# Projection loop of an RWKV block: the bonus products and each tile's last add move from VectorE to GpSimd

## The chip, the cores and the metric

The kernel runs on one core of a Trainium2 chip. The metric is the device time of one execution in microseconds (us); the median of three executions is compared.

## The reference

Two layers of a diffusion transformer for 256 latent and 256 context tokens of width 1024: each layer is half a feed-forward block, a mixer, and a second half of a feed-forward block. The first layer's mixer is RWKV-7, in two directions. What matters here is how its inputs for the scan and for the readout come from the projections:

```
k = xk @ wk;  v = xv @ wv
kk = to_heads(k * k_k);  kk = kk / max(||kk||, 1e-12)
a = sigmoid(a0 + (xa @ a1) @ a2);  g = sigmoid(xg @ g1) @ g2     # for each direction
k_d = k * (1 + (a - 1) * k_a)
...
bonus = sum(r * k_d * r_k, axis=head) * v
out   = (yn * ln_w + ln_b + bonus) * g
```

The second layer's mixer is grouped attention; it lies outside of the change.

## The kernel before

All activations are held as 128 channels by 512 tokens (256 of the context, 256 latent), so a matrix of 1024 channels is eight tiles. Matrices are split into two parts of float32r, and each product is three matmuls (function `mm3`, lines 268 to 270). The split is a copy by ScalarE (`whi`, L260) and a subtraction by VectorE (`wlo`, L261).

The stage that is changed is `rwkv_project` (L656). Its loop has nine turns, `ct` from 0 to 8, and is pipelined by hand: turn `ct` makes the gates, the key and the decay sums of tile `ct` (`gates`, `key`, `sums`), and finishes tile `ct - 1` (`mixed`, `value`). For ScalarE the order is that of the code; the instructions of the other engines are placed by the framework's planner, so on VectorE and TensorE pieces of two turns are interleaved. Each engine then works through its own queue strictly in that order.

What the steps of one turn do, with the lines used below:

- `sums`: two cumulative sums (VectorE, `cum`, L743), two exponentials `p` and `pin` for each direction (ScalarE, L748 and L750), two one-column memsets and two one-column copies of 8 elements, `pc<-p`, by GpSimd (L747, L751), and a DMA of `pc` (L752).
- `mixed`: VectorE forms `kk` (L758), `b` (L763), the scan's operands `ar` (L768, L769), `kd` (L775), the bonus product `pr` = kd x r for each direction (L777), and `bk` (L778, L779). DMAs write `ar` (`far`, L771) and `bk` (`fbk`, L780, L783) to DRAM.
- `value`: the product with wv and the gates' second product (TensorE, `pp`, `gp`), copies of v by ScalarE (L803, L806, L814), DMAs of v (`fv`, L808) and of the gates (`fgl`, L816). Then, for each direction, TensorE sums the bonus product over each head (`bop`, L819, which has `pr` as its moving operand), VectorE multiplies by v (L821) and applies bias and gate (L822). The two directions are added (L824), and the sum goes to DRAM (`bg`, L825).

All DMA writes of this loop, and the load of r (`load_r`, L707), are issued by GpSimd (`put = nc.gpsimd`, L698). The buffer of `ar` is also that of v's copies (pool `f1`, one buffer, tag "ar", L764 and L804), so `ar` of the next tile can't be written before `fv` has left it, and v's copies can't be made before `far` has left it. `r`, `k`, `sq` and `kk` of a tile lie in the same eight pieces as the results of `value`: L821 of direction 0 overwrites `r`. In the last turn (`ct` = 8) the triangular solve of the scan's first tile (`early_solve`, L955; its VectorE steps are L919 to L938) is interleaved with `mixed` and `value`, and the scan stage begins when it is done.

Of the kernel before, what the change touches and what calls it, by code (L numbers as in the profile page):

```python
# [12 lines left out]
ALU = mybir.AluOpType  # L13
# [75 lines left out]
class Net:  # L89
# [566 lines left out]
    def rwkv_project(self):  # L656
        nc, a = self.nc, self.a
# [3 lines left out]
        with ExitStack() as st:  # L661
# [5 lines left out]
            def ft(nm="ft"):  # L667
                return f.tile([128, 520], F32, tag="f", name=nm)[:, 0:T]
# [4 lines left out]
            def fl(p):  # L673
                return p.rearrange("p h t -> p (h t)")

            def o4(t):
                return t.rearrange("p (h c i) -> p h c i", h=2, c=4)

            def o8(t):
                return t.rearrange("p (h c) i -> p h c i", h=2)  # L680
# [4 lines left out]
            def hmm(w, slot, hslot, q0, q1):  # L685

                return (tuple(u[q0:q1, slot] for u in w), tuple(self.hid(HID0 + hslot)[q0:q1, :, i] for i in range(2)))
# [66 lines left out]
            def mixed(ct, bc):  # L754

                z = zs[ct]
                kt, rt, kkt, p65, pin = (z[q] for q in ("k", "r", "kk", "p65", "pin"))
                nc.vector.scalar_tensor_tensor(  # L758
                    out=kkt, in0=kt, scalar=self.vec[:, V_KK, ct:ct + 1], in1=bc, op0=ALU.mult, op1=ALU.mult)
                b = {}  # L760
                for d in range(2):
                    b[d] = ft("b")
                    nc.vector.tensor_tensor(out=o4(b[d]), in0=self.order(kkt, d), in1=o4(z[W_A, d]), op=ALU.mult)  # L763
                ar = f1.tile([128, 2, 2, 4, 2, 64], F32, tag="ar", name="ar")  # L764
                bk = f1.tile([128, 2, 2, 4, 2, 64], F32, tag="bk", name="bk")
                for d in range(2):
                    kk, r = (self.order(q, d) for q in (kkt, rt))
                    nc.vector.tensor_tensor(out=ar[:, :, d, :, 0], in0=kk, in1=o8(p65[d][:, :, 0:64]), op=ALU.mult)  # L768
                    nc.vector.tensor_tensor(out=ar[:, :, d, :, 1], in0=r, in1=o8(p65[d][:, :, 1:65]), op=ALU.mult)  # L769
                    if d:  # L770
                        put.dma_start(  # L771
                            out=self.far[ct].rearrange("p f d x -> p (f d x)"), in_=ar.rearrange("p f d c s i -> p (f d c s i)"))
                    k = self.order(kt, d)
                    kd = ft("kd")
                    nc.vector.tensor_tensor(out=o4(kd), in0=o4(z["asg", d]), in1=k, op=ALU.mult)  # L775
                    pr = z["pr", d] = ft("pr")
                    nc.vector.tensor_tensor(out=self.order(pr, d), in0=o4(kd), in1=r, op=ALU.mult)  # L777
                    nc.vector.tensor_tensor(out=bk[:, :, d, :, 1], in0=o4(b[d]), in1=o4(pin[d]), op=ALU.mult)  # L778
                    nc.vector.tensor_tensor(out=bk[:, :, d, :, 0], in0=o4(kd), in1=o4(pin[d]), op=ALU.mult)  # L779
                put.dma_start(  # L780
                    out=self.fbk[ct, 0:64].rearrange("p f c s i -> p (f c s i)"), in_=bk[0:64].rearrange("p f d c s i -> p (f d c s i)"))
                for e in range(2):
                    put.dma_start(  # L783
                        out=self.fbk[ct, 64:128].rearrange("p f c s i -> p (f c) s i")[:, :, 1 - e],
                        in_=bk[64:128].rearrange("p f d c s i -> p (f d c) s i")[:, :, e])
# [9 lines left out]
            def value(ct):  # L795
                z = zs[ct]
                own, w = z["own"], z["wg"]
                rkb = f2.tile([128, 128], F32, tag="rkb", name="rkb")
                nc.vector.tensor_scalar(
                    out=rkb, in0=cst[:, C_BO:C_BO + 128], scalar1=self.vec[:, V_RK, ct:ct + 1], scalar2=None, op0=ALU.mult)  # L800
                p = self.product(z["wv"], hlv, BOTH, "pp")
                v = own[0]
                nc.scalar.activation(out=v, in_=fl(p), func=AF.Copy)  # L803
                v2 = f1.tile([128, 2, 2, CTX], F32, tag="ar", name="v2")  # L804
                for d in range(2):
                    nc.scalar.activation(  # L806
                        out=v2[:, :, d].rearrange("p f (c i) -> p f c i", c=4), in_=self.order(v, d), func=AF.Copy)
                put.dma_start(out=self.fv[ct], in_=v2)  # L808
                gs = []
                for d in range(2):  # L810
                    p = self.pmm.tile([128, 2, CTX], F32, tag="mm", name="gp")
                    self.mm3(p, [hmm(w, d, W_GA + d, 0, 128), hmm(w, 2, W_GC, 32 * d, 32 * d + 32)])
                    gl = own[6 + d]
                    nc.scalar.activation(out=gl, in_=fl(p), func=AF.Copy, scale=self.vec[:, V_LW + d, ct:ct + 1])  # L814
                    gs.append(p)
                put.dma_start(out=self.fgl[ct], in_=pieces[:, 8 * (ct % 2) + 6:8 * (ct % 2) + 8])  # L816
                for d in range(2):
                    p = self.pmm.tile([128, T], F32, tag="mm", name="bop")
                    nc.tensor.matmul(out=p, lhsT=rkb, rhs=z["pr", d], start=True, stop=True)  # L819
                    t = own[4 + d]  # L820
                    nc.vector.tensor_tensor(out=t, in0=v, in1=p, op=ALU.mult)  # L821
                    nc.vector.scalar_tensor_tensor(  # L822
                        out=t, in0=t, scalar=self.vec[:, V_LB + d, ct:ct + 1], in1=fl(gs[d]), op0=ALU.add, op1=ALU.mult)
                nc.vector.tensor_tensor(out=own[4], in0=own[4], in1=own[5], op=ALU.add)  # L824
                put.dma_start(out=self.bg[ct], in_=own[4])  # L825

            with self.tc.manual_schedule(engines={mybir.EngineType.Activation}):
# [4 lines left out]
                for ct in range(KT + 1):  # L832
# [25 lines left out]
                    if ct:  # L858
                        mixed(ct - 1, bc)
                    if ct + 1 < KT:  # L860
                        load(ct + 1)
                    if ct:
                        value(ct - 1)
# [820 lines left out]
```

## Time and profile before

| | us |
|---|---|
| median of 3 executions | 2347.47 (2346.8 to 2347.53) |
| the profiled execution | 2345.08 |
| its span | 2343.3 |
| mean granted TensorE clock | 0.953 |
| the changed loop, in the span | some 575 to 762 |

The profile is of one execution. TensorE is busy for 93% of the span, VectorE for 65%, ScalarE for 46% and GpSimd for 7%; the last is nearly all in the changed loop and the scan behind it. Times in the rows are microseconds from the start of the span, durations of single instructions are in us or, where marked, ns. An instruction's span on GpSimd is rough, and it contains the time in which the instruction is held.

### The profile page before, as it was taken

The numbers are of one execution on the slowest core, as the hardware profiler recorded it, in microseconds if no ns is written. First come the engines' busy times: TensorE is split into PE (matmuls) and PEld (weight loads), VectorE is DVE, ScalarE is ACT, GpSimd is POOL, SyncE is SP. The second block draws the span as 40 slices with busy tenths as digits, with TensorE's granted clock in tenths as the row PEclk, the third lists the DMA queues.
The fourth block names the chain that finished last, engine by engine and source line by source line (L and its number), as shares of the span: only waits on it lengthen the run. The fifth ranks groups of instructions, "written<-read, shape, count | busy, mean of one in ns | idle before, by whom it ended". The sixth has DMA issues, their size and how long they took to land.

```text
span 2343.3 us, 44872 instructions
## 1 busy us (share of the span) xinstructions
PE 2184.3 (93%) x18548; PEld 1866.8 (80%) x18548; DVE 1515.0 (65%) x2609; ACT 1073.4 (46%) x1912; POOL 156.3 (7%) x224
## 2 busy tenths in 40 slices
PE   6999999897997899998999999989999999998998
PEld 4777889665775788776997788988778898678997
DVE  3798325566888667574699732579983367775554
ACT  3222325445884555555652222564222365555443
POOL 0000000000453222220000000000000000000000
PEclk9999999898998889998999999999999999798999
DMA  7567336542676534332577533567763464103664
GB/s 260 190 219 227 99 99 194 159 142 72 211 260 208 180 99 131 96 103 79 162 232 227 179 99 90 173 193 244 226 197 96 117 179 125 55 20 119 186 178 137
DMA packets 105004, 366.78 MB, mean 157 GB/s; under 512 B 13920, under 2 KB 16224, under 8 KB 102112
## 3 DMA queue, kind: packets, MB, share of 16 engines
q1 hardware_dynamic: 93024, 319.81, 43.6%
q0 software_dynamic: 11776, 44.12, 6.1%
q8 instruction: 145, 2.38, 0.4%
q14 instruction: 59, 0.48, 0.1%
HBM read 331.30 MB, written 32.57 MB: 155 GB/s over the span
## 4 chain that ended last, share of the span: by engine, by line
PE 51%; DVE 11%; DMA 5%; ACT 5%; issue 4%; POOL 1%; DVEq 0%; ACTq 0%; SPq 0%; POOLq 0%
PE h L270 5%; PE h L268 5%; PE h L269 5%; PE yps L270 4%; PE yps L268 4%; PE yps L269 4%; DMA y<-in_modt 3%; DVE junk L222 3%; DVE wlo L261 3%; PE scp L907 2%; PE cpl L1115 1%; PE op L1548 1%; PE sp L1267 1%; DMA fgl<-yx 1%; PE up L1251 1%
## 5 line engine op out<-in xcount | busy, mean ns | idle before, releaser
L260 ACT ACTIVATE whi<-wp 128x1024 fp32r<-128x1024 f32 (+1 forms) x396 | 409.3, 1034 | 737.0 <-PE h L269 381.9
L261 DVE TENSOR_TENSOR wlo<-wp,whi 128x1024 fp32r<-128x1024 f32 (+1 forms) x396 | 471.5, 1191 | 383.8 <-ACT whi L260 378.4
L270 PE MATMUL h<-nh,wlo 128*128 128x512 f32 (+1 forms) x1520 | 525.7, 347 | 16.6 <-DVE wlo L261 15.9
L268 PE MATMUL h<-nh,whi 128*128 128x512 f32 (+1 forms) x1520 | 524.0, 345 | 8.1 <-ACT whi L260 6.6
L269 PE MATMUL h<-nh,whi 128*128 128x512 f32 (+1 forms) x1520 | 522.9, 345 | 0.0
L270 PEld LDWEIGHTS h<-nh,wlo 128*128 128x128 f32 x1520 | 290.2, 191 | 61.6 <-DVE wlo L261 27.7
L268 PEld LDWEIGHTS h<-nh,whi 128*128 128x128 f32 x1520 | 290.8, 192 | 42.1 <-ACT whi L260 8.2
L269 PEld LDWEIGHTS h<-nh,whi 128*128 128x128 f32 x1520 | 290.6, 191 | 33.6
L270 PE MATMUL yps<-hidB,wlo 128*128 128x256 f32 (+1 forms) x658 | 199.7, 303 | 1.4 <-DVE wlo L261 1.4
L268 PE MATMUL yps<-hidB,whi 128*128 128x256 f32 (+1 forms) x658 | 200.2, 304 | 0.0
L269 PE MATMUL yps<-hidB,whi 128*128 128x256 f32 (+1 forms) x658 | 199.9, 304 | 0.0
L222 DVE SCALAR_TENSOR_TENSOR junk<-y 128x1024 bf16<-128x1024 f32 x144 | 176.0, 1222 | 17.2 <-DMA y<-in_modt 15.0
L270 PEld LDWEIGHTS yps<-hidB,wlo 128*128 128x128 f32 x658 | 125.6, 191 | 6.5 <-DVE wlo L261 1.6
L269 PEld LDWEIGHTS yps<-hidB,whi 128*128 128x128 f32 x658 | 125.7, 191 | 4.9
L268 PEld LDWEIGHTS yps<-hidB,whi 128*128 128x128 f32 x658 | 125.7, 191 | 4.9
L413 DVE TENSOR_TENSOR gg<-s,h 128x512 f32<-128x512 f32 (+1 forms) x98 | 56.0, 571 | 95.3 <-PE h L270 93.2
L270 PE MATMUL yps<-hidA,wlo 128*128 128x256 f32 (+1 forms) x376 | 114.5, 305 | 0.5 <-DVE wlo L261 0.5
L268 PE MATMUL yps<-hidA,whi 128*128 128x256 f32 (+1 forms) x376 | 114.0, 303 | 0.0
L269 PE MATMUL yps<-hidA,whi 128*128 128x256 f32 (+1 forms) x376 | 114.0, 303 | 0.0
L222 DVE SCALAR_TENSOR_TENSOR junk<-dw,cb 128x1024 bf16<-128x1024 f32 x80 | 97.9, 1223 | 16.2 <-DMA dw<-in_modt 11.3
L270 PEld LDWEIGHTS yps<-hidA,wlo 128*128 128x128 f32 x376 | 71.8, 191 | 4.0 <-DVE wlo L261 1.1
L269 PEld LDWEIGHTS yps<-hidA,whi 128*128 128x128 f32 x376 | 71.8, 191 | 2.9
(352 smaller groups left out, 3936.1 us busy)
## 6 DMA issues: line engine op xcount, KB each, us to landing
wp<-in_w SPq DMA_DIRECT2D x243, 512.0 KB, 3.6
wp<-in_w SPq DMA_DIRECT2D x94, 448.0 KB, 3.4
y<-in_modt SPq DMA_DIRECT2D x72, 512.0 KB, 4.4
dw<-in_modt SPq DMA_DIRECT2D x40, 512.0 KB, 4.2
wp<-in_wrkv SPq DMA_DIRECT2D x40, 512.0 KB, 4.0
mw<-in_modw SPq DMA_DIRECT2D x32, 512.0 KB, 4.5
far<-ar POOLq DMA_DIRECT2D x8, 1024.0 KB, 6.0
bk<-fbk SPq DMA_DIRECT2D x15, 512.0 KB, 3.8
```

What stands on the lines that cost most here:

```text
L222: nc.vector.scalar_tensor_tensor(out=junk, in0=ws[i % len(ws)], scalar=1.0, in1=cb[:, s], op0=ALU.mult, op1=ALU.mult, accum_out=self.mod[l ...
L260: nc.scalar.activation(out=hi, in_=raw, func=AF.Copy)
L261: nc.vector.tensor_tensor(out=lo, in0=raw, in1=hi.bitcast(F32), op=ALU.subtract)
L268: nc.tensor.matmul(out=ps, lhsT=wh, rhs=vh, start=first and j == 0, stop=False)
L269: nc.tensor.matmul(out=ps, lhsT=wh, rhs=vl, start=False, stop=False)
L270: nc.tensor.matmul(out=ps, lhsT=wl, rhs=vh, start=False, stop=last and j == n - 1)
L413: nc.vector.tensor_tensor(out=gg, in0=s1, in1=ps[1], op=ALU.mult)
L907: self.nc.tensor.matmul(out=p[h][:, c], lhsT=bk[q:q + 64, d, c], rhs=ar[q:q + 64, d, c].rearrange("p s i -> p (s i)"), start=True, stop=Tr ...
L1115: nc.tensor.matmul(out=p[hf][q:q + 32, u], lhsT=lhs(8 * hf + u, q), rhs=rhs[q:q + 32, 8 * hf + u], start=True, stop=True, tile_position=(q ...
L1251: nc.tensor.matmul(out=p[w:w + 64, d], lhsT=tt[:, d, c, w:w + 64], rhs=rt[:, d], start=True, stop=True, tile_position=(0, w))
L1267: nc.tensor.matmul(out=sp[q:q + 64, d], lhsT=bkt[:, d, c, h], rhs=uv[:, d, c, h], start=S is None and d == 0, stop=True, tile_position=(0, ...
L1548: nc.tensor.matmul(out=self.op.rearrange("p g q -> p (g q)"), lhsT=v2[:, b, i, pr, e].rearrange("p f d -> p (f d)"), rhs=pt[:, b, j].rearr ...
```

## The change

The two bonus products of each tile (L777) and the one addition at the end of each tile (L824) are issued to GpSimd instead of VectorE. Nothing else is edited. Seen over eight tiles, 16 multiplications and 8 additions of 128x512 float32 elements change their engine; all their operands lie in SBUF.

```
-                    nc.vector.tensor_tensor(out=self.order(pr, d), in0=o4(kd), in1=r, op=ALU.mult)
+                    nc.gpsimd.tensor_tensor(out=self.order(pr, d), in0=o4(kd), in1=r, op=ALU.mult)
...
-                nc.vector.tensor_tensor(out=own[4], in0=own[4], in1=own[5], op=ALU.add)
+                nc.gpsimd.tensor_tensor(out=own[4], in0=own[4], in1=own[5], op=ALU.add)
                 put.dma_start(out=self.bg[ct], in_=own[4])
```

## Rows read from the trace of the kernel before

**Rows 1.** The page, part 1: busy time by engine, whole span.

```profile
PE 2184.3 (93%) x18548; PEld 1866.8 (80%) x18548; DVE 1515.0 (65%) x2609; ACT 1073.4 (46%) x1912; POOL 156.3 (7%) x224
```

**Rows 2.** Busy time by stretch, about one turn: PE, PEld, DVE, ACT, POOL, clock, DMA.

```profile
688.00:710.00 22.00, 21.55 (x96) 15.32 (x94) 19.20 (x32) 18.31 (x27) 12.07 (x15) 1.00 0.75 257
```

**Rows 3.** Timeline of DVE, loop: start, duration, instruction, idle time before and its releaser.

```profile
623.96 1.39 DVE L821 TENSOR_TENSOR yx<-yx,bop 128x512 f32<-128x512 f32 x2
...
643.38 1.21 DVE L261 TENSOR_TENSOR wlo<-wp,whi 128x1024 fp32r<-128x1024 f32 x1
...
659.24 0.68 DVE L775 TENSOR_TENSOR kd<-asg,yx 128x512 f32<-128x512 f32 x1
...
660.45 0.68 DVE L777 TENSOR_TENSOR pr<-kd,yx 128x512 f32<-128x512 f32 x1
...
664.39 1.22 DVE L261 TENSOR_TENSOR wlo<-wp,whi 128x1024 fp32r<-128x1024 f32 x1
665.53 1.41 DVE L821 TENSOR_TENSOR yx<-yx,bop 128x512 f32<-128x512 f32 x2
...
669.56 0.69 DVE L769 TENSOR_TENSOR ar<-yx,p 128x512 f32<-128x512 f32 x1 [1.23 <-DMA fv<-v]
...
672.68 0.75 DVE L758 SCALAR_TENSOR_TENSOR yx<-yx,vec,bc 128x512 f32<-128x512 f32 x1 [0.56 <-PE bc L888]
...
706.48 1.41 DVE L821 TENSOR_TENSOR yx<-yx,bop 128x512 f32<-128x512 f32 x2
...
712.05 0.69 DVE L769 TENSOR_TENSOR ar<-yx,p 128x512 f32<-128x512 f32 x1 [2.77 <-issue]
```

**Rows 4.** Timeline of PE, loop.

```profile
651.64 0.66 PE L888 MATMUL bc<-cst,yx 128*128 128x128 f32 x4 [0.86 <-DVE yx L880]
...
664.25 1.96 PE L819 MATMUL bop<-pr,rkb 128*128 128x512 f32 x4
...
714.47 0.66 PE L888 MATMUL bc<-cst,yx 128*128 128x128 f32 x4 [1.73 <-DVE yx L880]
```

**Rows 5.** Timeline of POOL, loop.

```profile
597.91 0.47 POOL L751 COPY pc<-p 128x8 f32<-128x8 f32 x1 [7.25 <-ACT p L748]
...
639.17 5.47 POOL L751 COPY pc<-p 128x8 f32<-128x8 f32 x1 [2.65 <-ACT p L748]
...
666.62 0.54 POOL L808 DMA_DIRECT2D fv<-v  x1
...
669.25 0.64 POOL L816 DMA_DIRECT2D fgl<-yx  x1
...
676.53 0.54 POOL L771 DMA_DIRECT2D far<-ar  x1 [4.82 <-DVE ar L768]
```

**Rows 6.** Waits in 575 to 765: waiter, releaser, total us, times, longest us.

```profile
DVE ar L769 <- DMA fv<-v: 6.1, 4, 1.9
```

**Rows 7.** Instructions of two lines: count, duration in ns min/median/max, first and last start.

```profile
L751 POOL COPY pc<-p x16: 186/670/6252, 580.6 to 727.0; 128x8 f32<-128x8 f32 x16
L824 DVE TENSOR_TENSOR yx<-yx x8: 683/686/691, 607.3 to 760.3; 128x512 f32<-128x512 f32 x8
```

**Rows 8.** Groups of POOL by line: count, busy us, mean ns, idle before.

```profile
L974 POOL MEMSET early<- 128x256 f32 x1 | 0.3, 312 | 2.9 <-PE scp L907 2.9
L975 POOL MEMSET early<- 128x16 f32 x1 | 0.1, 127 | 0.1
```

**Rows 9.** Busy time by stretch of 3 us, columns as in Rows 2.

```profile
726.00:729.00 3.00, 3.00 (x13) 1.80 (x12) 1.29 (x3) 0.00 (x0) 1.70 (x3) 0.78 0.98 408
729.00:732.00 3.00, 3.00 (x26) 1.78 (x26) 1.38 (x3) 2.08 (x4) 0.54 (x1) 0.66 0.16 61
```

**Rows 10.** Timelines of DVE and POOL, last turn.

```profile
752.86 1.49 DVE L821 TENSOR_TENSOR yx<-yx,bop 128x512 f32<-128x512 f32 x2 [1.60 <-PE bop L819]
...
760.30 0.69 DVE L824 TENSOR_TENSOR yx<-yx 128x512 f32<-128x512 f32 x1
...
749.16 0.54 POOL L771 DMA_DIRECT2D far<-ar  x1 [8.24 <-DVE ar L769]
```

## The prediction

> **What bounds the kernel now.** I read the page's busy shares first: TensorE is busy for 93% of the span, GpSimd for 7% [rows 1]. That average hides the stage of the change, so the next view is the busy time by stretch: in one turn of the loop TensorE is busy for 21.55 of 22 us at full clock, VectorE for 19.20, GpSimd for 12.07 [rows 2]. Two engines are nearly full, and the third is far from idle, since it issues all of the loop's DMA writes. Next, the timeline of VectorE: L821 of the first and the fifth full turn start at 623.96 and 706.48 [rows 3], so four turns take 82.52 us, 20.63 each. TensorE's only idle time in a turn is ahead of the transposes `bc`: 0.41, 0.86, 0.19, 0.45 and 1.73 us in five turns, 3.64 in all (the second and the last are shown) [rows 4]. VectorE's idle time has two places: it waits for the DMA `fv` to leave the buffer that `ar` needs (1.23 us in the turn shown; 6.1 us in four turns, and 2.77 in a fifth, where the view names no releaser) and for `bc` (0.56) [rows 3, 6]. So a turn is held by TensorE with almost no slack, and beside it by a ring through VectorE, GpSimd's queue and a DMA.
>
> The view that decides is GpSimd's timeline. Its copy of 8 elements a partition, `pc<-p`, takes 0.47 us at 597.91 but 5.47 us at 639.17 [rows 5]; over 16 of them the durations go from 186 to 6252 ns [rows 7]. The long one ends at 644.64, and VectorE's `wlo`, the last of an unbroken run of instructions with two SBUF operands, ends at 643.38 + 1.21 = 644.59 [rows 3]; behind it comes L821, which has one operand in PSUM. This pattern stands in six of the eight tiles that have these copies: the first copy of the pair ends within 0.1 us of the end of VectorE's run, the second takes 0.19 us. I read it so: a GpSimd instruction that reads SBUF doesn't get in between VectorE's two-operand instructions while these follow each other without a gap, and all that is behind it in GpSimd's queue (the DMAs `fpc`, `fv`, `fbk`, `fgl`) waits too.
>
> The Trainium skill says of this, in "SBUF — State Buffer", section "Who interferes with whom", that a VectorE instruction with two SBUF inputs contends with a GpSimd instruction that reads SBUF, and that whoever issues first holds the shared ports for its whole instruction. By its letter GpSimd would get in at the next boundary between two instructions; the copy at 597.91 agrees with that, the copy at 639.17 doesn't, and the difference is the first rival below.
>
> **The change, part by part.**
>
> *Removed from VectorE.* Two products and one add in each turn. One of them lasts 0.69 us [rows 7], but instructions overlap: kd at 659.24 and pr two places later at 660.45 give 0.60 us a place [rows 3]. So 1.2 us leave the run that ends with `wlo`, and 0.6 us leave the part behind L822: 1.8 us a turn.
>
> *Added to GpSimd.* No row shows a GpSimd instruction with two operands. Its memsets give a pace: 127 ns for 16 elements and 312 for 256 [rows 8], 0.77 ns an element, so a mere write of 512 takes 0.13 + 0.38 = 0.51 us. That is the lower bound. The upper bound is the shortest copy, 186 ns for 8 elements [rows 7], which, if all above a memset of that size (some 0.13 us) went by element, would give 0.13 + 512 x 0.0066 = 3.5 us. I take 1.3 us, an estimate: two reads and a write at the memset's pace, 0.13 + 3 x 0.38, since the memset is the nearest row in size.
>
> The skill's "GPSIMD Engine Reference", section "Elementwise — side-by-side cycle accounting", gives 4497 ns for a two-input add of 2048 elements; in proportion that is an estimate of 1.1 us here, and with it the sum below would be some 2 us smaller.
>
> *Where the products wait.* `pr` of direction 0 is ready to start when kd is done, in the middle of VectorE's run, as the copies are now. I let it wait for the end of that run, T. In the queue then come the rest of the copies (T + 0.2), pr 0 (T + 1.5), pr 1 (T + 2.8), and only then `fpc`, `fv`, `fbk`, `fgl`. Now `fv` is issued at 666.62, when T is 665.61, and VectorE goes on with L769 at 669.56, T + 3.95 [rows 3, 5]. All of that moves by 2 x 1.3 = 2.6 us. L821 must wait for `bop`, which waits for pr, and direction 0 also for pr 1 (it overwrites r): L821 at T + 2.8 and T + 3.9, L822 done near T + 6, still ahead of the L769 that waits for `fv` at T + 6.55. So `fv`, not `bop`, is the last wait. `fgl` moves from 669.25 [rows 5] by 2.6 us too, and ScalarE's next key work with it; kd starts without a wait at 659.24 [rows 3], and VectorE itself comes to it 2.0 us later (2.6 less the add), so this costs nothing unless its slack now is under 0.6 us.
>
> *Sum of a turn.* +2.6 (`fv`) - 0.6 (the add) - 1.2 (the products) = +0.8 us. It applies to the five full turns from 624 to 707: +4.0. In the turn before (copies at 597.91) nothing is starved and VectorE idles 2 us for `bop`: 0. In the turn after, ScalarE waits for a late DMA of `far`: 0, between -0.6 and +0.7.
>
> *The add.* It is queued behind `fgl`, near T + 7, and gets in while VectorE waits 0.56 us for `bc` ahead of L758 [rows 3], whose second operand lies in PSUM. Nothing behind it is urgent: `bg`, then `far`, which VectorE releases 4.8 us later [rows 5]. Cost 0, as long as that gap is there.
>
> *The last turn.* pr 0 waits for the end of the run, 752.86 - 1.60 [rows 10] - 1.2 = 750.06; it ends at 751.36; `far` (now issued at 749.16) is queued behind it, then pr 1 until 753.2, `bop` (half of 1.96 us [rows 4]) until 754.2: the second L821 is 0.65 us later than now. VectorE saves the add, 0.6 [rows 10], but GpSimd's add now meets the solve's small two-operand steps and may hold them for 0 to 1.3 us; I take half. Together +0.7.
>
> *TensorE's clock.* A turn of 20.63 + 0.8 with some 20.15 us of TensorE work has 1.3 us of idle time. Turns with up to 0.86 us keep clock 1.00; the one with 1.73 us [rows 4] is followed, 12 us later, by a stretch with 0.78 and 0.66, that is partly at 1.2 GHz: 3 x 0.22 + 3 x 0.34 = 1.7 us lost [rows 9]. I charge that once, +1.7; none to all five turns is 0 to +8.5.
>
> Sum: 4.0 + 0 + 0.7 + 1.7 = +6.4 us. The profiled execution would go from 2345.08 to 2351.5. The median lies 2.39 us above the profiled execution, so I forecast 2353.9, +0.27%. What measurement can tell from no change is about 0.2%, 4.7 us.
>
> **The rivals.**
>
> *First: GpSimd gets in at instruction boundaries.* Then VectorE is held for 2 x 1.3 and saves 1.8, +0.8 of work a turn, but the copies and `fv` are early and its 8.87 us of waits in five turns (6.1 + 2.77) go: -1.0 a turn. TensorE then bounds, and only its 3.64 us of idle time [rows 4] can be won: 2343.8, faster by less than 0.2%. For it: the copy at 597.91 [rows 5]. Against: six of eight tiles.
>
> *Second: GpSimd's product is cheap* (0.51 us). `fv` moves by 1.0, a turn gains 0.8 until TensorE bounds it: -3.6, and -1 in the last turn, 2342.9, on the edge of faster. The memset speaks for the pace, the missing reads against it.
>
> *Third: the planner places things otherwise.* With `bop` behind the next gates' matmuls, or `fv` ahead of pr, the waits are covered, and the two engines' balance gives -5 to +3: about 2346.
>
> *Fourth: the add misses the gap ahead of L758.* Then it is starved through the whole run, some 13 us, and `far` and `load_r` are behind it. `far` now is issued at 676.53 [rows 5]; issued after the next T, its buffer comes free some 9 us late for v's copies, and `fv` behind them: 5.4 us a turn more, +27 in five: 2381. It decides if GpSimd comes to the add more than 2.5 us later than I think.
>
> **How the numbers follow.** Forecast 0.56 (slower 0.44, same 0.12, since without a clock loss it is +4.7); first rival 0.13 (faster 0.03, same 0.10); second 0.09 (faster 0.06, same 0.03); third 0.13 (faster 0.05, same 0.07, slower 0.01); fourth 0.09, slower. Faster 0.14, same 0.32, slower 0.54. The range leaves out the fourth and half of the second: low 2343.5; high 2366, the forecast with the clock's loss in all five turns (+6.8) and a product of 1.8 us (+5.0). The far bound of 3.5 us for a product would give 2 x 2.2 a turn more, +22, and is left out with the fourth.
>
> **What would show it.** Right: L777 and the add on GpSimd with spans up to 5 us in the loop, ending 1.3 us or more after VectorE's run; L769 waiting for `fv` for some 3 us; `bop` with idle time ahead of it on TensorE; turns of 21.4 us. Wrong: turns under 20.6; pr done before the run ends; VectorE's products next to them stretched to 1.3 us (the first rival); `far` issued behind the add by more than 5 us (the fourth).

## The result: 1.3% slower, most of it in the projection loop

The median goes from 2347.5 to 2378.97 us; the ratio on record is 1.0127, 95% interval [1.009, 1.0165] (the two medians alone would give 1.0134). The forecast was 2353.9 us, with a range from 2343.5 to 2366: the direction was right, the size was not.

The profiled execution of the changed kernel took 2379.28 us, with a span of 2377.5 (before: 2345.08 and 2343.3). To see where the 34.2 us are, I cut both spans at three instructions that they share: the first prefix sum of the projection (L743), the scan's first transposition (L1161) and the first matmul into `yo`, behind the scan.

| stage (us) | before | after | difference |
|---|---|---|---|
| up to the first L743 | 576.9 | 576.8 | -0.1 |
| projection, to the first L1161 | 192.7 | 216.6 | +23.9 |
| scan, to the first matmul into `yo` | 335.2 | 345.3 | +10.1 |
| the rest | 1238.5 | 1238.8 | +0.3 |

Busy time by stretch, first of the kernel before, then of the changed one, for the scan and the projection. The columns are the stretch, its length, busy time and instruction count of PE, PEld, DVE, ACT and POOL, then the granted clock, the DMA share and GB/s.

```profile
769.63:1104.86 335.23, 309.07 (x7537) 261.17 (x7537) 204.03 (x519) 175.59 (x498) 71.06 (x108) 0.90 0.37 108
576.90:769.63 192.73, 166.89 (x747) 120.42 (x746) 164.22 (x282) 132.76 (x200) 83.69 (x108) 0.92 0.66 223
```

```profile
793.37:1138.70 345.33, 319.57 (x7536) 270.70 (x7536) 204.50 (x519) 176.22 (x499) 71.42 (x110) 0.87 0.36 107
576.90:793.37 216.47, 178.07 (x746) 121.75 (x746) 159.78 (x257) 131.60 (x199) 108.26 (x131) 0.85 0.60 195
```

In the scan only TensorE's busy time moved: 10.5 us more for the same matmuls, at a clock of 0.87 for 0.90. In the projection two things stand side by side. TensorE is busy 11.2 us longer with the same matmuls, at a clock of 0.85 for 0.92, and idle 12.6 us longer (38.4 for 25.8). VectorE has 4.4 us less to do, GpSimd 24.6 us more.

One steady turn, in the rows that answer to [rows 3 to 5]. The first fence is VectorE's timeline, the second GpSimd's, the third TensorE's with two stretches of its clock (columns: length, PE busy, clock, DMA share, GB/s).

```profile
652.86 1.23 DVE L261 TENSOR_TENSOR wlo<-wp,whi 128x1024 fp32r<-128x1024 f32 x1 [0.35 <-ACT whi L260]
658.52 0.69 DVE L821 TENSOR_TENSOR yx<-yx,bop 128x512 f32<-128x512 f32 x1 [4.43 <-PE bop L819]
659.98 0.69 DVE L821 TENSOR_TENSOR yx<-yx,bop 128x512 f32<-128x512 f32 x1 [0.77 <-PE bop L819]
...
661.98 0.69 DVE L769 TENSOR_TENSOR ar<-yx,p 128x512 f32<-128x512 f32 x1
662.58 0.20 DVE L736 RECIPROCAL hrs<-hrs 128x8 f32<-128x8 f32 x1
662.69 1.67 DVE L769 TENSOR_TENSOR ar<-yx,p 128x512 f32<-128x512 f32 x1
...
665.46 0.75 DVE L758 SCALAR_TENSOR_TENSOR yx<-yx,vec,bc 128x512 f32<-128x512 f32 x1 [0.56 <-PE bc L888]
...
672.36 0.69 DVE L775 TENSOR_TENSOR kd<-asg,yx 128x512 f32<-128x512 f32 x1
...
676.75 1.23 DVE L261 TENSOR_TENSOR wlo<-wp,whi 128x1024 fp32r<-128x1024 f32 x1 [0.35 <-ACT whi L260]
682.40 0.69 DVE L821 TENSOR_TENSOR yx<-yx,bop 128x512 f32<-128x512 f32 x1 [4.43 <-PE bop L819]
```

```profile
650.07 2.50 POOL L751 COPY pc<-p 128x8 f32<-128x8 f32 x1 [3.39 <-ACT p L748]
652.51 0.54 POOL L707 DMA_DIRECT2D yx<-dr  x1
653.05 1.08 POOL L751 COPY pc<-p 128x8 f32<-128x8 f32 x1
654.43 0.54 POOL L752 DMA_DIRECT2D fpc<-pc  x1 [0.30 <-POOL pc L751]
654.98 1.28 POOL L777 TENSOR_TENSOR pr<-kd,yx 128x512 f32<-128x512 f32 x1
656.19 0.57 POOL L808 DMA_DIRECT2D fv<-v  x1
656.76 1.28 POOL L777 TENSOR_TENSOR pr<-kd,yx 128x512 f32<-128x512 f32 x1
...
662.14 1.68 POOL L824 TENSOR_TENSOR yx<-yx 128x512 f32<-128x512 f32 x1 [1.33 <-DVE hrs L735]
```

```profile
656.31 3.63 PE L819 MATMUL bop<-pr,rkb 128*128 128x512 f32 x4 [1.33 <-POOL pr L777]
```

```profile
678.00:681.00 3.00, 1.68 (x9) 0.84 0.47 162
681.00:684.00 3.00, 3.00 (x5) 0.59 0.83 262
```

Let T be the end of the second `wlo`, as in the prediction: 654.09. From there the reader follows the ring. GpSimd finishes the second product at T + 3.95. TensorE waits for the products and runs the four passes of `bop`, two for each direction, in 3.63 us (before: 1.96 [rows 4]). VectorE, which used to take L821 at T, waits for the first two for 4.43 us. Its second L821 waits for the other two, which need the second product, until T + 5.89. What stands behind it follows without a gap, and L769 starts at T + 7.89 with no wait for `fv` at all. The next T is 23.89 us on, the next L821 (682.40) 23.88. Cut at the same places, a turn is:

| part of a turn (us) | before | forecast | after |
|---|---|---|---|
| T to the first L769 | 3.95 | 6.55 | 7.89 |
| first L769 to L758 | 3.12 | 2.52 | 3.48 |
| L758 to the first kd | 6.91 | 6.91 | 6.90 |
| first kd to the next T | 6.37 | 5.17 | 5.62 |
| sum | 20.35 | 21.15 | 23.89 |

Between the L821 that open the turns the seven distances were 20.02, 20.55, 21.02, 20.35, 20.60, 22.21 and 24.18 us and are 25.64, 23.87, 23.88, 23.89, 23.90, 25.38 and 23.59. The stage's +23.9 is +5.2 ahead of the first of them, +5.6 in the first turn, +16.2 in the next five, -0.6 in the seventh and -2.5 behind it. The sixth, 25.38, has one more wait: the load of r stood for 2.64 us in GpSimd's queue, ahead of the products, until `bg` had landed. The waits of the changed kernel (575 to 800: total us, times, longest) name the releaser; in the kernel before, L821 waited for `bop` four times, 6.3 us in all:

```profile
DVE yx L821 <- PE bop L819: 37.1, 15, 7.8
PE bop L819 <- POOL pr L777: 14.2, 7, 3.7
```

### The profile page after: what moved, and what is told of

It reads as the page before. It is cut to its first block, busy times and chain, and to the rows that moved or that the text cites. A ratio compares the mean times of both kernels' runs of the same rounds, so it can differ in the third digit from the quotient of the medians.

```text
span 2377.5 us, 44856 instructions
## 1 busy us (share of the span) xinstructions
PE 2208.9 (93%) x18548; PEld 1881.7 (79%) x18548; DVE 1511.8 (64%) x2585; ACT 1073.0 (45%) x1912; POOL 181.3 (8%) x248
## 4 chain that ended last, share of the span: by engine, by line
PE 53%; DVE 11%; ACT 5%; issue 4%; DMA 4%; POOL 1%; DVEq 0%; ACTq 0%; SPq 0%; POOLq 0%
PE h L270 5%; PE h L268 5%; PE h L269 5%; PE yps L270 4%; PE yps L268 4%; PE yps L269 4%; DVE junk L222 3%; DMA y<-in_modt 3%; DVE wlo L261 2%; PE scp L907 1%; PE cpl L1115 1%; PE op L1548 1%; PE sp L1267 1%; PE pp L270 1%; PE bop L819 1%
```

## The experiments

Theory at the start: the products come late out of GpSimd's queue, and the turn waits for that. Rivals: the add does it; GpSimd slows VectorE through what the two share, whoever waits; TensorE's clock does it. All ratios are to the kernel before on the same chip; "stage" is the projection as cut above.

**Products alone, and the add alone.**

```diff
 e1: only L777 goes to nc.gpsimd
 e2: only L824 goes to nc.gpsimd
```

> The products are done by GpSimd, the last add stays with VectorE. Theory (the ring through the products: VectorE's run, GpSimd's queue, bop, L821): the turns from the third to the seventh stay near 23.5 us, against 23.9 changed and 20.6 before, since only the add's hold of L769 goes (1.67 instead of 0.64 us) and 0.6 us of add comes back. The projection stage (first cumulative sum to the scan's first transposition: 192.7 us before, 216.6 changed) takes 212 to 217. Rival (the add is what costs): turns near 20.6 to 21, the stage under 200.

> Only the last add of each tile is done by GpSimd. Theory of the ring through the products: the add falls beside VectorE's wait for fv (1.2 to 2.8 us a turn) and saves 0.6 us of VectorE behind it, at most holds one L769: turns of 20.2 to 21.0 us, the stage 190 to 196 us (before: 192.7). Rival (the add's hold costs 1 us a turn): turns of 21.6, the stage 199 or more.

The products alone: ratio 1.0102 [1.0072, 1.0132], stage 217.9 us, a little above the 212 to 217 expected, with turns of 23.88 to 23.89 where the loop is steady (two of seven; two others are 23.02 and 27.17). The add alone: 1.0024 [1.0005, 1.0044], stage 201.9, which is the rival's number (199 or more). The two don't add up: with the products on GpSimd, the steady turn is 23.89 with the add on either engine. So the loss is the products', and the add's price is covered by theirs. The add alone cost more than I gave it. In its longest turn (25.05 us) the load of r, which the planner had moved ahead of `fpc` and `fv`, waited 1.18 us for `bg` to land, and L821 then 3.40 us for `bop`; in the next turn an L769 lasted 1.67 us beside the add.

**A product that nobody needs.** VectorE keeps its products; GpSimd repeats 416 of the 512 elements into a tile that nobody reads.

```diff
                     nc.vector.tensor_tensor(out=self.order(pr, d), in0=o4(kd), in1=r, op=ALU.mult)
+                    nc.gpsimd.tensor_tensor(out=sh, in0=o4(kd)[:, :, :, 0:52], in1=r[:, :, :, 0:52], op=ALU.mult)
```

> VectorE computes the products as before and TensorE uses those; GpSimd computes 416 of the 512 elements of each product once more, into a bf16 tile that nobody reads (some 1.05 us each). This shows the delay of what is behind the products in GpSimd's queue, without anybody waiting for the products. The step of the prediction (fv goes later by both products): L769 waits 2.1 us longer, turns of 22.5 to 22.8 us, the stage near 203 us. If GpSimd's queue has slack there: turns of 20.6, the stage 193. The theory that the ring through bop is what made 23.9 needs this run to stay clearly under 23.9.

Ratio 1.013 [1.0109, 1.0151], stage 222.8: as slow as the change itself, though TensorE has its `pr` from VectorE in time. The expectation wanted turns clearly under 23.9 if the ring through `bop` is what counts. They are 23.32 to 27.16 us, but for the last, so by its own words this run speaks against that ring; it has another wait in its place. VectorE's and GpSimd's timelines show who waits:

```profile
662.41 1.28 DVE L821 TENSOR_TENSOR yx<-yx,bop 128x512 f32<-128x512 f32 x2 [3.75 <-POOL sh L777]
```

```profile
652.91 5.94 POOL L751 COPY pc<-p 128x8 f32<-128x8 f32 x2 [2.44 <-ACT p L748]
659.14 0.54 POOL L752 DMA_DIRECT2D fpc<-pc  x1 [0.29 <-POOL pc L751]
659.69 1.07 POOL L777 TENSOR_TENSOR sh<-kd,yx 128x416 bf16<-128x416 f32 x1
660.70 0.57 POOL L808 DMA_DIRECT2D fv<-v  x1
661.28 1.09 POOL L777 TENSOR_TENSOR sh<-kd,yx 128x416 bf16<-128x416 f32 x1
```

L821 of direction 0 writes its result over r, and GpSimd still reads r. The second product ends at 662.37, L821 starts at 662.41. So a late read of r is enough for such a loss. Whether r or `bop` comes last in the changed kernel is read from its own trace, further down. Here the wait could be the whole cost, or the sharing of memory could; the next kernel tells them apart.

**The same with no one waiting.** Both operands are kd, so that L821 may overwrite r at once. From the third turn on the order of VectorE's and of GpSimd's instructions is that of the kernel just shown.

```diff
-    nc.gpsimd.tensor_tensor(out=sh, in0=o4(kd)[:, :, :, 0:52], in1=r[:, :, :, 0:52], op=ALU.mult)
+    nc.gpsimd.tensor_tensor(out=sh, in0=o4(kd)[:, :, :, 0:52], in1=o4(kd)[:, :, :, 0:52], op=ALU.mult)
```

> The kernel before, and beside each bonus product of VectorE one of GpSimd of 416 of the 512 elements (1.08 us in the run before it) whose result nobody reads; this time both its operands are kd, so that nobody has to wait until GpSimd has read r. In the steady turns the order of VectorE's and GpSimd's instructions is that of the other shadow kernel. Theory A (a wait on GpSimd's late reading of r is what lengthens a turn, the two instructions in GpSimd's queue cost little by themselves): the first adds of a turn (L821) wait under 0.5 us, steady turns of 20.5 to 21.6 us, projection stage 194 to 203 us. Rival B (GpSimd's instructions slow VectorE through what the two engines share, whoever waits): turns of 23 us and more and a stage over 214 us, as with the other shadow kernel (222.8).

Ratio 1.0064 [1.0047, 1.0081], stage 202.9, 20 us less than its twin. The two differ in a little more than the wait: a product of kd with itself lasts 0.89 us for 1.07 to 1.10, and the first two turns have another order. Five turns of seven are 20.30, 20.74, 21.17, 21.17 and 20.37 us. In such a turn L821 starts at T again, and what is late is `fv`, as the prediction had it:

```profile
674.00 1.38 DVE L821 TENSOR_TENSOR yx<-yx,bop 128x512 f32<-128x512 f32 x2
678.85 0.69 DVE L769 TENSOR_TENSOR ar<-yx,p 128x512 f32<-128x512 f32 x1 [1.40 <-DMA fv<-v]
```

T is 672.86 + 1.21 = 674.07 here, so L769 starts at T + 4.78 for T + 3.95 before: +0.83 us, for one product of 0.89 us ahead of `fv`. The mechanism of the forecast exists and has the size that it was given; it is not what governs the change. The other two are 26.89 and 25.64 us, 6.3 and 3.4 more than the same turns before. In the first of these L769 waited 3.28 us for `fv`, TensorE stood idle for 3.73 us ahead of `bc`, and then ran at half clock:

```profile
634.00:638.00 4.00, 2.41 (x8) 0.50 0.83 274
638.00:642.00 4.00, 4.00 (x13) 0.64 0.59 184
```

**TensorE kept busy ahead of `bop`.** The changed kernel with filler matmuls whose results the real `bop` overwrites. My first form read a piece that ScalarE writes late, and the planner changed VectorE's order around it; its turns (22.4 to 29.4 us, ratio 1.0139 [1.0106, 1.0173]) tell nothing about the clock.

```diff
 e6:   before each bop
+      nc.tensor.matmul(out=p, lhsT=rkb, rhs=z["kk"], start=True, stop=True)
 e11b: before the first bop of a turn, twice
+      nc.tensor.matmul(out=p, lhsT=rkb, rhs=own[3], start=True, stop=True)
```

> The changed kernel, with one more matmul ahead of each bop: it multiplies the same weights by a tile that is ready early and writes the same PSUM tile, which bop then overwrites, so TensorE works while it waits for GpSimd's product. Theory that half clock after TensorE's idle time is a part of the ring: bop at full clock (the pair's span 3.6 us becomes 2 to 2.6), granted clock near 1.00 through the loop, turns of 22.8 to 23.3 us. If the clock is no part: turns of 23.9 or, since the added matmuls come ahead of bop, up to 24.9 us.

> The changed kernel with two more products of TensorE ahead of the first bop of a turn, on operands that are long there and into the same bank, which the real bop then overwrites; the order on VectorE and GpSimd is as in the changed kernel. They fill the 1.33 us that TensorE stands idle ahead of bop. Theory A (each turn loses time again because TensorE stands idle ahead of bop and then runs at half clock): the granted clock stays near 1.00 behind bop, where it was 0.59 over 681 to 684 us, and turns go from 23.9 to 22.2 to 23.3 us. Rival B (the half clock falls on work that has slack): the clock is restored and turns stay at 23.7 to 24.1 us. Rival C (the idle time that matters is another): the clock still falls, turns of 23.9 us and more.

The second form has the changed kernel's order on VectorE and GpSimd, and the clock is whole again. TensorE's stretches in the same places as above, then VectorE's L821 and the `bop` of the second direction:

```profile
678.00:681.00 3.00, 2.55 (x10) 1.00 0.83 262
681.00:684.00 3.00, 3.00 (x16) 1.00 0.89 197
```

```profile
678.81 0.69 DVE L821 TENSOR_TENSOR yx<-yx,bop 128x512 f32<-128x512 f32 x1 [4.00 <-POOL pr L777]
680.00 0.69 DVE L821 TENSOR_TENSOR yx<-yx,bop 128x512 f32<-128x512 f32 x1 [0.50 <-PE bop L819]
```

```profile
678.83 1.13 PE L819 MATMUL bop<-pr,rkb 128*128 128x512 f32 x2 [0.45 <-POOL pr L777]
```

Steady turns are 23.16 to 23.20 us instead of 23.89, and the stage is 211.2. So the half clock costs 0.7 us of a turn. What stays, 2.8 us over the 20.35 of before, begins at the end of GpSimd's second product, T + 3.97 (T is 674.81 here), for which both L821 wait. The first waits to T + 4.00, since that product reads the r that L821 overwrites. The second waits to T + 5.19, since TensorE starts the second direction's `bop` only when that product is there, and L769 follows the second, at T + 7.18. So the wait on r ends 1.2 us ahead of the last one: without it the second L821 would still stand at T + 5.19. That reading is the trace's; no run takes the wait on r out of the changed kernel. The whole did not gain measurably (1.0133 [1.0083, 1.0183]).

**The queue ahead of the products.** ScalarE computes the eight values of `pc` with an activation of its own, so that GpSimd has no copies: in the changed kernel (e4), in the kernel with the products alone (e10) and in the kernel before (e5).

```diff
-                    nc.gpsimd.tensor_copy(out=pc[:, d], in_=p65[:, :, 64])
+                    nc.scalar.activation(out=pc[:, d], in_=c8(cum[d])[:, :, 63], func=AF.Exp, scale=-LAM)
```

> The changed kernel, but the 8-element copies of L751 leave GpSimd: ScalarE computes the same 8 values by an activation of its own. Theory A (whatever GpSimd instruction stands first is held until VectorE's run of 12 two-input instructions has a gap): now the first product of a turn is held in their place, it lasts some 5 us instead of 1.28, but the 3 us of queue ahead of it (copy, load, copy, issue of fpc) are gone: L821 waits 1.2 to 2.5 us instead of 4.4, turns of 21 to 22.3 us, stage 199 to 207 us. Rival B (only the short copies are held, a 512-element product gets in at once): both products run at 1.28 us within the run, L821 does not wait, turns of 20.5 us or less, stage under 196 us. Rival C (the copies had no part in it): stage 214 to 218 us as in the changed kernel.

e4: ratio 1.0094 [1.0061, 1.0128], stage 216.8, which is the number of rival C, but not its reason. In one turn the first product did take the copies' place and was held for 4.16 us. In five others the load of r, which stands ahead of it, waited for `bg`: the add on GpSimd let the planner put `bg` behind `far`, and r's buffer is the one that `bg` reads. GpSimd's timeline and its waits:

```profile
626.17 4.16 POOL L777 TENSOR_TENSOR pr<-kd,yx 128x512 f32<-128x512 f32 x1
...
651.09 0.54 POOL L707 DMA_DIRECT2D yx<-dr  x1 [6.09 <-DMA bg<-yx]
```

```profile
POOL yx L707 <- DMA bg<-yx: 33.1, 5, 8.3
```

> Only the bonus products are on GpSimd, the add stays on VectorE, and the 8-element copies of L751 are done by ScalarE: the load of r, which in the run before it (copies on ScalarE, add on GpSimd) waited some 6 us for bg to land, then finds bg landed earlier. So the first product of a turn stands at the head of GpSimd's queue when its operands are there. Theory A (VectorE's run holds whatever GpSimd instruction comes first): the first product lasts 4 to 5.5 us in most turns, ends with the first gap of the run, L821 waits 1.2 to 2.5 us, turns of 21 to 22.3 us, stage 198 to 206 us. Rival B (a product of 512 elements gets in at once): products of 1.28 us inside the run, turns of 20.5 us or less, stage under 196 us. Rival C (the queue ahead of the products doesn't matter): stage 214 to 218 us, as with the products alone and the copies on GpSimd (217.9).

e10: ratio 1.0057 [1.0035, 1.0079], stage 207.2, turns of 21.95 to 22.77 in the loop's middle. That lies a little above A's numbers and far from C's: 10.8 us of the stage's loss with the products alone came from what stood ahead of them. A's reason did not come with its numbers: the first product was held in two of eight tiles only (4.14 and 5.25 us). In the loop's middle it is not held, but not early either, since the issue of `fpc` now waits for ScalarE. GpSimd's timeline, then VectorE's:

```profile
673.11 0.54 POOL L752 DMA_DIRECT2D fpc<-pc  x1 [4.89 <-ACT pc L751]
673.66 1.55 POOL L777 TENSOR_TENSOR pr<-kd,yx 128x512 f32<-128x512 f32 x1
676.03 0.57 POOL L808 DMA_DIRECT2D fv<-v  x1 [0.81 <-ACT v L806]
676.61 1.27 POOL L777 TENSOR_TENSOR pr<-kd,yx 128x512 f32<-128x512 f32 x1
```

```profile
674.10 2.19 DVE L261 TENSOR_TENSOR wlo<-wp,whi 128x1024 fp32r<-128x1024 f32 x1
677.92 0.69 DVE L821 TENSOR_TENSOR yx<-yx,bop 128x512 f32<-128x512 f32 x1 [1.62 <-POOL pr L777]
```

The second product ends at 677.88 and L821 starts at 677.92: the same ring, with 1.62 us of wait for 4.43. Beside the first product `wlo` lasts 2.19 us instead of 1.23.

> The kernel before with the 8-element copies of L751 taken from GpSimd to ScalarE in the same way; the order of VectorE's instructions is unchanged. Theory A (in the kernel before, the issue of fv stands behind the held copies and ends the last wait of most turns): fv is issued when its data are there, some 2 us earlier, and the wait of L769 on its landing (6.1 us in 4 turns) goes: stage 186 to 191 us instead of 192.7, the whole 2 to 6 us faster. Rival B (another wait stands close behind): stage 191.5 to 194 us, no change in the whole.

e5: L769's wait for `fv` falls from 6.1 us to 1.6 and the stage to 190.1, as theory A said. The whole does not: 0.9999 [0.998, 1.0018]. In the profiled execution the scan and the rest took 6 us more than in the kernel before.

**The scan.** The kernel before, with 64 multiplications by 1.0 on VectorE ahead of the scan, which change no value.

```diff
+    [nc.vector.tensor_scalar(out=self.early["td"], in0=self.early["td"], scalar1=1.0, scalar2=None, op0=ALU.mult) for _ in range(64)]
```

> The kernel before with 64 multiplications by 1.0 on VectorE between the projection and the scan (some 22 us), which change no value: the scan starts later by as much as in the changed kernel, with the same instructions behind it. Theory A (the scan's 10 us in the changed kernel are a matter of when it starts and what clock it is then granted): scan of 340 us and more instead of 335.2, with the sum of window length times granted clock still 307 to 310 us. Rival B (the change itself costs time in the scan): scan of 334 to 337 us, the whole later by about 22 us only.

Ratio 1.0129 [1.0106, 1.0153]. The scan took 340.7 us at a clock of 0.88, without any change in the loop:

```profile
795.90:1136.59 340.69, 314.29 (x7537) 265.94 (x7537) 204.25 (x519) 173.23 (x497) 67.74 (x103) 0.88 0.35 103
```

So a scan of over 340 us needs no GpSimd products. But a late start doesn't set its length either: with the products alone it started at 794.8, in the changed kernel at 793.4, and took 337.2 and 345.3 us. Over twelve profiled executions with the same instructions in the scan it took 335 to 348 us, and the longest have the lowest clocks. The product of length and clock, which I had put at 307 to 310 us, is 300 here (340.69 x 0.88). What sets the scan's clock stays open, and so does whether its 10 us belong to the change.

## Why the prediction was wrong, point by point

- **What bounds the loop.** The two views were read rightly: TensorE has almost no slack, and a ring through VectorE and GpSimd's queue lies beside it. The ring named was the wrong one.
- **The price of a product.** 1.3 us was taken; 16 products have a median of 1.276 us. The rival of the cheap product (0.51) is out, and so is the far bound of 3.5.
- **GpSimd held by VectorE's run.** Right for whatever stands first: 5.65 us for a copy at 623.86, 5.25 us for the first product of the last turn. In the steady turns it broke down in part. VectorE, with two products less, reaches `wlo` before its `whi` is there, and in that gap of 0.35 us the copy gets in (650.07 to 652.57). The first rival (GpSimd gets in at any boundary) is refuted by the held ones.
- **The order of the queue: the step that failed first.** I let the products follow the copies and put `fpc` and `fv` behind both. In the changed kernel the load of r, a copy, `fpc` and the first product lie between T - 1.6 and T + 2.2, then `fv`, then the second product. It ends at T + 3.95 instead of T + 2.8, while `fv` is issued only 1.1 us later than before, not 2.6.
- **"`fv`, not `bop`, is the last wait": the step that decided.** L821 was put at T + 2.8 and T + 3.9; it came at T + 4.43 and T + 5.89, and L769, which I let wait for `fv` until T + 6.55, at T + 7.89 without any such wait. So `bop` is the last wait: the second product, then its half of `bop`, then the second L821. `fv` was issued at T + 2.10; with the 2.94 us from its issue to L769 in the kernel before [rows 3, 5], it would have let L769 go near T + 5.0 (an estimate). The prediction had both of L821's waits, for `bop` and for the r that it overwrites, and covered both with `fv`. The pair of unread products shows, for r, that it takes such a wait and not only GpSimd's products beside VectorE: with the wait the stage is 222.8 us, without it 202.9.
- **The four terms of a turn.** Forecast +0.8, measured +3.54 in a steady turn. The missing 2.74 us are 1.34 up to L769, 0.96 from L769 to L758, and 0.45 in VectorE's run. Of the 1.34, 0.71 is the half clock, since without it L769 started at T + 7.18 (681.99 in the kernel with the filler), and 0.63 is the queue. The 0.96 is the add: its saving of 0.6 was booked, but the second L769 lasted 1.67 us for 0.64 beside it. The 0.45 are mostly the wait for `whi`, 0.35.
- **The add at nothing.** It came at T + 8.05, a microsecond later than I put it and beside the second L769 rather than in the gap ahead of L758; the fourth rival, an add that starves, did not come, and that its 2381 us lies near the measured time is chance. But taking it back gained nothing beside the products, so the 0.96 is not a price that can be summed: with the add on VectorE, L821 and `bc` were waited for longer instead (4.58 and 0.98 us for 4.43 and 0.56).
- **TensorE's clock: one term mis-sized.** 1.7 us once, with +8.5 as the end of the range. TensorE idles ahead of `bop` and runs at half clock behind it in every steady turn. Its matmuls in the stage took 11.2 us more. In steady turns the filler won 0.7 us of 23.89 back, in the whole stage 5.4 us (216.6 to 211.2), which lies within the 0 to +8.5 that the prediction gave as bounds.
- **The turn with the copies at 597.91, at nothing: wrong by 5.2 us** of the stage's 23.9, the part ahead of the first L821. The planner's rival came true with the other sign. It put the key's factor (L735 at 605.01 to L758) ahead of L821 (609.01); the two products held `l2l` for 3.14 us; and TensorE, idle, ran at half clock. I did not try these by themselves. The 5.6 us of the next turn are another matter: 5.19 of them are the ring's wait, L821 at 634.65 for `bop`, behind a copy that was held until 629.51 and a second product that ended at 634.17. VectorE's row and TensorE's stretches of the changed kernel, ahead of the first L821:

```profile
599.77 3.14 DVE L261 TENSOR_TENSOR l2l<-l2r,l2h 128x256 fp32r<-128x256 f32 x1 [0.82 <-ACT l2h L260]
```

```profile
604.00:608.00 4.00, 1.92 (x6) 0.62 0.94 235
608.00:612.00 4.00, 4.00 (x10) 0.53 0.93 311
```

- **The last turn at +0.7: wrong.** The first product was held for 5.25 us, as said. But the seventh turn, put at 0 between -0.6 and +0.7, became 0.6 us shorter, and what follows, which has the +0.7, 2.5 us shorter; the planner had put L919 ahead of L821 there. I did not try that by itself.
- **The scan at nothing:** 10 us more in the profiled execution, left open above.

## What to carry to other kernels

When work moves to another engine, follow the tile that it writes to the last instruction that needs it, and every tile that it reads to the next one that overwrites it: here the first chain, through `bop`, ended last, and with products that nobody needs the second alone made the stage as long. Write down the queue in the order in which the new engine will really come to it, DMA issues and loads included, before giving the moved work a time. And where TensorE has no slack, price each new idle place twice, once as idle time and once as the half clock that may follow, in every turn that has it.

## What the runs showed of the hardware

- VectorE and GpSimd hold each other, both ways. Beside a GpSimd instruction of 128x512 a VectorE instruction with two SBUF operands stretched from 0.64 to 1.67 us (L769), from 1.23 to 2.19 (`wlo`), from 0.41 to 3.14 beside two (`l2l`). The other way a product lasted 4.16 and 5.25 us for 1.28; each ended some 1.1 us after the last instruction of VectorE's two-operand run. The Trainium skill, "SBUF — State Buffer", section "Who interferes with whom", says that whoever issues first holds the shared ports for its whole instruction. The first three agree; the last two don't, as by that sentence the product would have got in at the next boundary, some 0.6 us on.
- The same GpSimd product of 416 elements took 1.07 to 1.10 us with kd and r (14 of 16) and mostly 0.89 with kd twice.
- Filling 1.33 us of TensorE's idle time ahead of `bop` with matmuls on data that nobody needs brought the granted clock from 0.59 to 1.00 in the stretch behind it.
